# Loading the index queries ahead of the retention values, and preparing them one step sooner

## Chip, cores and metric

One core of one Trainium2 chip. The metric is the device time of one execution in microseconds (us), the median of several runs. A profiled execution gives the trace; times in it are counted from the start of its span.

## What is computed

One block of a language model on 512 tokens and 16 meta tokens (T = 528), width 1024, all in float32: a gated feed-forward layer, a mixer and a second feed-forward layer, each with a residual and a norm ahead of it. The mixer has two branches, a retention branch (4 heads, key width 256, value width 512) and a sparse attention branch (8 heads). In the sparse branch an index picks 128 keys for each query. The index is what is edited:

```python
def hybrid_mixer(u, pos, k_top, w_in, w_ret_out, w_att_out, w_mix_out):
    proj = u @ w_in
    rq, rk, rv, rg, aq, ak, av, iq, ik, iw, g_ret, g_att = jnp.split(proj, offs, axis=-1)
    ...
    yr = (jax.nn.silu(rg) * retention(rope(rq), rope(rk), rv)) @ w_ret_out
    iq = rope(iq.reshape(B, T, IDX_HEADS, IDX_DH), pos)      # 8 heads of 64
    ik = rope(ik.reshape(B, T, 1, IDX_DH), pos)[:, :, 0]
    ya = dsa_attention(aq, ak, av, iq, ik, iw, k_top).reshape(B, T, ATT_W) @ w_att_out
    merged = jax.nn.sigmoid(g_ret) * yr + jax.nn.sigmoid(g_att) * ya
    return merged @ w_mix_out

# in dsa_attention, for a block of queries:
    rel = jax.nn.relu(jnp.einsum('bqhd,bsd->bqhs', qib, ki))
    score = jnp.einsum('bqh,bqhs->bqs', wib, rel) * idx_scale
    _, sel = lax.top_k(score, k_top)
```

## The kernel before

Every product is made of three matmuls: both operands are split into a high and a low part (`hi`, `lo`), and high by high, high by low and low by high are summed. ACT makes the high part (a copy with rounding), DVE the low part (a subtraction). So each weight tile costs a load, an ACT split (`whi`) and a DVE split (`wlo`) before PE can use it.

The retention stage is one list of steps, run by `steps_through`. A step has a load, a tile of weights and a run. At step i the loop issues the load of step i+4, the ACT split of step i+2, and then the run of step i: its matmuls, then `lower()` (the DVE split of step i+2), then `behind(ps)` (what is done with the result). PE, ACT and DVE follow this written order; a scheduler orders the instructions of SP and POOL, which issue the transfers. Weight splits have three buffers, raw weights two (each two tiles), and the PSUM pool `sm` four banks.

The steps around the change are, in order:

- four gate tiles of head 0 (`psrg`; `gates_of(0)`). `behind_0` to `behind_3` apply silu; `behind_1` also computes head 0's decayed score matrix (`decayed(0)`, matmuls `psst`); `behind_1` to `behind_3` prepare the index queries; `behind_3` splits head 0's values (`values_in(0)`).
- two `psrq` tiles and two `psrk` tiles of head 1 (`queries_keys(1)`). `q0` prepares the index keys. `weigh(0, c)` multiplies values and score matrix (matmuls `pspv`), and DVE and ACT make `to`, `sq` and `ossum` from the result. `pair` calls put the index's own matmuls (`pssc`) between those of the projections.

The index queries wait in DRAM (`fq`). `bring_index`, called ahead of the first gate tile, loads them to `ia` (SP), and with the two halves of each head exchanged to `ib` (POOL, four pieces); it also loads the rope tables `cosi` and `sini`, head 0's values (four blocks, tile `vraw`), the index keys, the value tails and the causal mask. `index_queries(i)` has four parts:

- 0 multiplies `ia` by the cosine, 1 multiplies `ib` by the sine (DVE, 128 x 1536 each),
- 2 adds them (DVE) and copies the high parts to `iqx` (ACT, two copies of 64 x 1536),
- 3 subtracts for the low parts (DVE, two of 64 x 1536).

`index_keys(0)` to `(2)` are the same for the keys, with 64 x 512 elements. `ia` and `ib` share the memory of the value parts (`vo0`, `vo1`), so the values can be split only once the index queries are done. In the trace both appear as `ixs`.

Of the kernel before, what the change touches and what calls it, by code (L numbers as in the profile page):

```python
# [11 lines left out]
F32 = mybir.dt.float32  # L12
# [6 lines left out]
P = 128  # L19
D = 1024  # L20
KD = D // P
S = 512
# [59 lines left out]
def kernel(ctx: ExitStack, tc: tile.TileContext, x, meta, g1, wg1, wu1, wd1, gm,  # L82
                      w_in, w_ro, w_ao, w_mo, g2, wg2, wu2, wd2, gf, rope, decay, causal, out):
    nc = tc.nc
# [195 lines left out]
    vst = dpool.tile([6, P, 4, 4, P], F32, name="vst")  # L280
# [281 lines left out]
    if True:  # L562
# [120 lines left out]
        with tc.manual_schedule(engines={mybir.EngineType.PE, mybir.EngineType.Activation, mybir.EngineType.DVE}):  # L683
# [38 lines left out]
            second = [turned(1, (0,))]  # L722
# [66 lines left out]
        with tc.manual_schedule(engines=BUSY):  # L789
# [9 lines left out]
            raw = load_w(wg1[:, 2 * P : 4 * P], KD, 2 * P)  # L799
            w = split_w(raw[:, :, :P])  # L800
# [9 lines left out]
            w = split_w(raw[:, :, P:])  # L810
# [5 lines left out]
            lower = s1.hidden(0, pr)  # L816
            raw = load_w(wu1[:, 2 * P : 4 * P], KD, 2 * P)
# [3 lines left out]
            w = split_w(raw[:, :, :P])  # L821
# [6 lines left out]
            w = split_w(raw[:, :, P:])  # L828
# [58 lines left out]
        first, second = slice(0, 2 * P), slice(2 * P, 4 * P)  # L887
# [324 lines left out]
        with tc.manual_schedule(engines=BUSY):  # L1212
            pr = s1.spare("l", "pr")
            nc.vector.tensor_tensor(pr[:, 0, :], halves(psus[0])[1], st[0], ALU.mult)
            lower = s1.hidden(2, pr[:, 0, :], (0,))
# [156 lines left out]
    if True:  # L1372
# [4 lines left out]

        def bring_index():
            new_decay(0)
            heads[0]["raw"] = [rt.tile([P, S], F32, tag="to", name="vraw", bufs=4) for _ in range(4)]  # L1380
            for c in range(4):
                nc.sync.dma_start(heads[0]["raw"][c], vst[0, :, c].rearrange("p b d -> p (b d)"))
            nc.sync.dma_start(ia[:, :, :NL], fq[:, :, :NL])
            for r in range(4):
                o = r ^ 1
                nc.gpsimd.dma_start(ib[32 * r : 32 * r + 32, :, :NL], fq[32 * o : 32 * o + 32, :, :NL])
            for i, t in enumerate((cosi, sini)):
                nc.sync.dma_start(t, rope[0, i, :, REAL])
            nc.gpsimd.dma_start(ka[:64, :S], fs[:64, 0, :])
            for r in range(2):  # L1390
                nc.gpsimd.dma_start(kb_[32 * r : 32 * r + 32, :S], fs[32 * (1 - r) : 32 * (2 - r), 0, :])
            nc.gpsimd.dma_start(iw, fs[64 : 64 + IH, 0, :])
            place_tails(0)
            nc.sync.dma_start(caus, causal)
            for i, t in enumerate((cos, sin)):
                nc.sync.dma_start(t, rope[2, i])
# [5 lines left out]
        def index_queries(i):  # L1402
            late = slice(P, S)
            a, b = ia[:, :, :NL], ib[:, :, :NL]
            if i < 2:
                t, tb = ((a, cosi), (b, sini))[i]
                TT(t, t, tb[:, late].unsqueeze(1).to_broadcast([P, 4, NL]), ALU.mult)
            elif i == 2:
                TT(a, a, b, ALU.add)
                for r, own, far in sides_of:  # L1410
                    nc.scalar.activation(iqx[own, r::2, :], a[own], AF.Copy)
            else:
                for r, own, far in sides_of:
                    TT(iqx[far, r::2, :], a[own], iqx[own, r::2, :].bitcast(F32), ALU.subtract)

        def index_keys(i):
            a, b = ka[:64, :S], kb_[:64, :S]
            if i == 0:
                TT(a, a, cosi[:64], ALU.mult)
                TT(b, b, sini[:64], ALU.mult)  # L1420
            elif i == 1:
                TT(a, a, b, ALU.add)
                for r in (0, 64):
                    nc.scalar.activation(ikh[r : r + 64], a, AF.Copy)
            else:
                for r in (0, 64):
                    TT(ikl[r : r + 64], a, ikh[r : r + 64].bitcast(F32), ALU.subtract)
# [6 lines left out]
        def values_in(h):  # L1434
            if not vr.get("parts"):
                vr["parts"] = [rt.tile([P, 4, S], F32R, tag=f"vo{i}", name="vo") for i in range(2)]
            parts, raw = vr["parts"], heads[h]["raw"]
            if h == 0:
                lows = [in_two(raw[c], *(p[:, c, :] for p in parts)) for c in range(4)]
            else:  # L1440
                lows = [in_two(raw[:, c : c + 2], *(p[:, c : c + 2, :] for p in parts)) for c in (0, 2)]
            heads[h]["vs"] = [(parts[0][:, c, :], parts[1][:, c, :], tp["v"][:TR, c * P : (c + 1) * P]) for c in range(4)]
            for low in lows:
                low()
# [164 lines left out]
        def gates_of(h):  # L1609

            p = h - 1

            def behind_0(ps):
                silu(h, ps)
                if h:
                    norm_diag(p)
                    if h > 1:
                        pick(2)

            def behind_1(ps):  # L1620
                silu(h, ps)
                if h == 0:
                    decayed(0)
                    index_queries(0)
                else:
                    two_normed_parts(p, 0)

            def behind_2(ps):
                silu(h, ps)
                if h == 0:  # L1630
                    index_queries(1)
                    index_queries(2)
                elif h == 1:
                    two_normed_parts(p, 2)
                else:
                    pick(1)

            def behind_3(ps):
                silu(h, ps)
                if h == 0:  # L1640
                    index_queries(3)
                    values_in(0)
                    picks["pairs"] = index_steps()
                    picks["steps"] = select_steps()
                elif h == 1:
                    for _ in picks["pairs"]:
                        pass
                else:
                    if h == RH - 1:
                        weigh(h, 0)  # L1650
                    pick(3)

            sums, spread = (6, lambda: norm_sums(p)), (4, lambda: norm_all(p))
            inside = [()] * 4
            if h == 1:
                inside = [((2, pair), (4, pair), sums), ((1, pair), spread, (6, pair)), ((4, pair), (7, pair)),
                          ((4, pair),)]
            elif h:
                inside = [(sums,), ((4, lambda: pick(1)), (7, lambda: norm_all(p))), ((2, lambda: two_normed_parts(p, 2)),), ()]
            runs = [proj("psrg", REAL, i, b) for i, b in zip(inside, (behind_0, behind_1, behind_2, behind_3))]  # L1660
            if h == 0:
                run0 = runs[0]

                def first(w, lower):
                    bring_index()
                    run0(w, lower)

                runs[0] = first
            c0 = OFF_RG + h * DV
            if h < RH - 1:  # L1670
                return steps_of(tiles(("rg", h), w_in, c0, 4), runs)
            return steps_of(tiles(("rg", h), w_in, c0, 3) + tiles("rg3", w_in, c0 + 3 * P, 1), runs)

        def queries_keys(h):

            pss, p = {}, h - 1
            ropes = heads[h]["ropes"] = {}

            def q0(ps):
                pss["qa"] = ps  # L1680
                if h == 1:
                    for i in range(3):
                        index_keys(i)
                else:
                    weigh(p, 0)
                    pick(1)

            def q1(ps):
                pss["qb"] = ps
                ropes["q"] = rope_pieces(pss["qa"], ps, cos[:, REAL], sin[:, REAL], S, ret_q)  # L1690
                if h == 1:
                    weigh(p, 0)
                some(ropes["q"], 5)
                weigh(p, 1)
                if h > 1:
                    pick(1)

            def k0(ps):
                pss["ka"] = ps
                some(ropes["q"], 1)  # L1700
                weigh(p, 2)
                some(ropes["q"], 1)
                if h > 1:
                    pick(2)

            def k1(ps):
                ropes["k"] = rope_pieces(pss["ka"], ps, cos, sin, T, ret_k)
                weigh(p, 3)
                if h > 1:
                    pick(2)  # L1710

            inside = ((2, pair), (4, pair), (6, pair)) if h == 1 else ()
            return (steps_of(tiles(("rq", h), w_in, OFF_RQ + h * DK, 2), [proj("psrq", REAL, ((5, pair),) if h == 1 else (), q0), proj("psrq", REAL, (), q1)])
                    + steps_of(tiles(("rk", h), w_in, OFF_RK + h * DK, 2), [proj("psrk", None, (), k0), proj("psrk", None, inside, k1)]))

# [52 lines left out]
        p = RH - 1  # L1768
# [69 lines left out]
        raw = vr["raw"]  # L1838
# [465 lines left out]
```

## Time and profile before

| | |
|---|---|
| median of 3 runs | 1520.0 us (1519.72 to 1521.01) |
| the profiled execution | 1520.12 us, of which the span is 1518.3 us |
| PE busy | 1507.0 us (99%) |
| DVE busy | 1095.7 us (72%) |
| ACT busy | 722.2 us (48%) |
| POOL busy | 104.6 us (7%) |
| transfers | 173.48 MB, 114 GB/s over the span |

A row of a timeline has the start in us, the duration in us, the engine, the line of the kernel, the operation and its tiles, and in brackets the idle time of the engine just ahead of it with what ended that. A row of the waits has who waited, for whom, the sum in us, how often, and the longest. A row of the transfers has the issuing queue, the count, the size of each and the us from issue to landing. `SPq` and `POOLq` are the queues of SyncE and GpSimd.

### The profile page before, as it was taken

How to read it: one execution, taken by the hardware profiler on the slowest of the kernel's cores; microseconds unless marked ns; L12 is line 12 of the kernel's file. 1: busy time of each engine (PE TensorE's matmuls, PEld its weight loads, DVE VectorE, ACT ScalarE, POOL GpSimd, SP SyncE). 2: the span in 40 equal slices, each digit the busy share in tenths (PEclk: the TensorE clock that was granted, in tenths of full speed). 3: DMA queues.
4: the chain of work that ended last, by engine and by line, in shares of the span. 5: the costliest groups of instructions: out<-in, count | busy, mean ns of one | idle time of the engine just before them, and what ended most of it. 6: DMA issues, size and time to landing. Idle time of an engine off the chain costs nothing. (4 is left out here: it accounts for less than half of the span.)

```text
span 1518.3 us, 23905 instructions
## 1 busy us (share of the span) xinstructions
PE 1507.0 (99%) x9764; PEld 1370.3 (90%) x9764; DVE 1095.7 (72%) x1701; ACT 722.2 (48%) x1126; POOL 104.6 (7%) x136
## 2 busy tenths in 40 slices
PE   9999999999999999999999999999999999999997
PEld 8999999999988888889898888998888899899996
DVE  4988586786886767787878787666455888586675
ACT  5655263454354444543324357666344445254453
POOL 1000000003101120000000131110001000000000
PEclk9999999999999999999999999999999999999999
DMA  5232323226554444232322343333443223233232
GB/s 169 59 122 88 117 90 111 89 93 209 195 165 161 167 147 141 87 122 86 106 88 85 97 123 89 79 90 105 151 131 128 84 84 108 87 112 111 84 124 85
DMA packets 151741, 173.48 MB, mean 114 GB/s; under 512 B 4944, under 2 KB 123240, under 8 KB 150992
## 3 DMA queue, kind: packets, MB, share of 16 engines
q1 hardware_dynamic: 142992, 151.58, 31.8%
q0 software_dynamic: 3808, 11.38, 2.0%
q10 hardware_dynamic: 4832, 9.00, 1.7%
q8 instruction: 76, 1.25, 0.3%
q14 instruction: 33, 0.27, 0.1%
HBM read 155.94 MB, written 16.01 MB: 113 GB/s over the span
## 5 line engine op out<-in xcount | busy, mean ns | idle before, releaser
L303 ACT ACTIVATE whi<-raw 128x1024 fp32r<-128x1024 f32 (+2 forms) x184 | 169.8, 924 | 130.2 <-PE psd L157 37.3
L304 DVE TENSOR_TENSOR wlo<-raw,whi 128x1024 fp32r<-128x1024 f32 (+2 forms) x184 | 198.5, 1083 | 44.9 <-ACT whi L303 44.9
L157 PE MATMUL psqX<-tl,whi 128*128 128x264 f32 (+1 forms) x432 | 122.3, 283 | 0.0
L157 PE MATMUL psqX<-th,whi 128*128 128x264 f32 (+1 forms) x432 | 122.3, 283 | 0.0
L157 PE MATMUL psqX<-th,wlo 128*128 128x264 f32 (+1 forms) x432 | 122.2, 283 | 0.0
L118 DVE TENSOR_TENSOR wlo<-raw,whi 128x1024 fp32r<-128x1024 f32 (+1 forms) x60 | 73.6, 1226 | 54.3 <-ACT whi L117 51.8
L303 ACT ACTIVATE whi<-wsum 128x1024 fp32r<-128x1024 f32 x72 | 76.3, 1060 | 70.7 <-PE psd L2139 22.0
L117 ACT ACTIVATE whi<-raw 128x1024 fp32r<-128x1024 f32 (+1 forms) x60 | 62.3, 1043 | 87.5 <-PE psat L157 26.6
L304 DVE TENSOR_TENSOR wlo<-wsum,whi 128x1024 fp32r<-128x1024 f32 x72 | 87.7, 1219 | 12.5 <-ACT whi L303 12.5
L157 PEld LDWEIGHTS psqX<-th,whi 128*128 128x128 f32 x432 | 82.1, 190 | 0.1
L157 PEld LDWEIGHTS psqX<-th,wlo 128*128 128x128 f32 x432 | 82.0, 190 | 0.0
L157 PEld LDWEIGHTS psqX<-tl,whi 128*128 128x128 f32 x432 | 82.0, 190 | 0.0
L157 PE MATMUL psro<-vo,whi 128*128 128x512 f32 x256 | 78.8, 389 | 0.0
L157 PE MATMUL psd<-hl,whi 128*128 128x264 f32 x352 | 71.4, 284 | 0.0
L157 PE MATMUL psd<-hh,wlo 128*128 128x264 f32 x352 | 70.8, 283 | 0.0
L157 PE MATMUL psd<-hh,whi 128*128 128x264 f32 x352 | 70.6, 282 | 0.0
L2139 PE MATMUL psd<-wlo,hh 128*128 128x512 f32 (+1 forms) x182 | 69.3, 382 | 0.0
L2139 PE MATMUL psd<-whi,hh 128*128 128x512 f32 (+1 forms) x182 | 69.2, 382 | 0.0
L2139 PE MATMUL psd<-whi,hl 128*128 128x512 f32 (+1 forms) x182 | 69.2, 382 | 0.0
L157 PEld LDWEIGHTS psro<-vo,whi 128*128 128x128 f32 x256 | 48.1, 188 | 10.0
L157 PEld LDWEIGHTS psd<-hh,wlo 128*128 128x128 f32 x352 | 54.5, 188 | 0.0
L157 PEld LDWEIGHTS psd<-hh,whi 128*128 128x128 f32 x352 | 54.1, 188 | 0.0
(447 smaller groups left out, 4511.6 us busy)
## 6 DMA issues: line engine op xcount, KB each, us to landing
raw<-in_ffn_w_up_dram SPq DMA_DIRECT2D x22, 1024.0 KB, 5.2
raw<-in_ffn_w_gate_dram SPq DMA_DIRECT2D x21, 1024.0 KB, 5.1
raw<-in_w_in_dram SPq DMA_DIRECT2D x18, 1024.0 KB, 5.1
raw<-in_w_in_dram SPq DMA_DIRECT2D x33, 512.0 KB, 3.7
raw<-in_ffn_w_down_dram SPq DMA_DIRECT2D x24, 512.0 KB, 4.5
w<-in_w_in_dram SPq DMA_DIRECT2D x24, 512.0 KB, 6.3
raw<-in_ffn_w_down_dram SPq DMA_DIRECT2D x12, 768.0 KB, 4.5
raw<-in_w_ret_out_dram SPq DMA_DIRECT2D x8, 1024.0 KB, 5.1
```

Of the source, the lines that this page charges most:

```text
L117: nc.scalar.activation(hi, src, AF.Copy)
L118: eng.tensor_tensor(lo, src, hi.bitcast(F32), ALU.subtract)
L157: nc.tensor.matmul(o, a[:, k, :], b[:, sl], start=first and k == 0 and i == 0, stop=last and k == nk - 1 and i == 2, skip_group_check=onto)
L303: nc.scalar.activation(hi, src, AF.Copy)
L304: return lambda: nc.vector.tensor_tensor(lo, src, hi.bitcast(F32), ALU.subtract)
L2139: nc.tensor.matmul(ps, a[:, bs], m[:, j, cs], start=first and i == 0, stop=last and i == 2)
```

## The change

Three things move; no instruction is added or removed.

- The loads of the values, the index keys and weights, the value tails, the mask and the retention rope tables go from `bring_index` to a new `bring_more`, called ahead of the second gate tile. `bring_index` keeps the decay table, the index queries and their rope tables.
- The index query parts move up: 1 from `behind_2` to `behind_1`, 3 from `behind_3` to `behind_2`.
- The first part of the index keys moves from `q0` to `behind_3`.

```diff
         def bring_index():
             new_decay(0)
-            heads[0]["raw"] = [rt.tile([P, S], F32, tag="to", name="vraw", bufs=4) for _ in range(4)]
-            for c in range(4):
-                nc.sync.dma_start(heads[0]["raw"][c], vst[0, :, c].rearrange("p b d -> p (b d)"))
             nc.sync.dma_start(ia[:, :, :NL], fq[:, :, :NL])
             for r in range(4):
                 o = r ^ 1
                 nc.gpsimd.dma_start(ib[32 * r : 32 * r + 32, :, :NL], fq[32 * o : 32 * o + 32, :, :NL])
             for i, t in enumerate((cosi, sini)):
                 nc.sync.dma_start(t, rope[0, i, :, REAL])
+
+        def bring_more():
+
+            heads[0]["raw"] = [rt.tile([P, S], F32, tag="to", name="vraw", bufs=4) for _ in range(4)]
+            for c in range(4):
+                nc.sync.dma_start(heads[0]["raw"][c], vst[0, :, c].rearrange("p b d -> p (b d)"))
             nc.gpsimd.dma_start(ka[:64, :S], fs[:64, 0, :])
...
                 if h == 0:
                     decayed(0)
                     index_queries(0)
+                    index_queries(1)
...
                 if h == 0:
-                    index_queries(1)
                     index_queries(2)
+                    index_queries(3)
...
                 if h == 0:
-                    index_queries(3)
                     values_in(0)
+                    index_keys(0)
                     picks["pairs"] = index_steps()
...
                     run0(w, lower)
 
                 runs[0] = first
+                run1 = runs[1]
+
+                def second(w, lower):
+                    bring_more()
+                    run1(w, lower)
+
+                runs[1] = second
...
                 if h == 1:
-                    for i in range(3):
+                    for i in range(1, 3):
                         index_keys(i)
```

## The prediction

> **What bounds the kernel now.** I read the engine totals first, then who waited for whom on PE around the change, then PE, DVE and ACT in order of time there, then the transfers and their landing times.
>
> ```profile
> span 1518.3 us, 23905 instructions
> PE 1507.0 (99%) x9764; PEld 1370.3 (90%) x9764; DVE 1095.7 (72%) x1701; ACT 722.2 (48%) x1126; POOL 104.6 (7%) x136
> PE pssc L1290 <- ACT sq L271: 1.6, 1, 1.6
> PE psrq L157 <- DVE wlo L304: 0.5, 1, 0.5
> ```
>
> PE is busy for 99% of the span. The change cannot take matmuls away, so it can win only where PE stands still. These two waits lie in the stage that is edited; the only other one that the profile names on PE is at the kernel's first matmuls. Here they are on PE, with a start of the first `rq` tile and a regular pair ahead of them:
>
> ```profile
> 580.31 0.39 PE L157 MATMUL psrq<-xh,wlo 128*128 128x512 f32 x1
> 585.57 0.39 PE L157 MATMUL psrq<-xh,wlo 128*128 128x512 f32 x1
> 585.80 0.41 PE L157 MATMUL psrq<-xh,whi 128*128 128x512 f32 x1
> 586.05 0.39 PE L157 MATMUL psrq<-xl,whi 128*128 128x512 f32 x1
> 586.97 0.50 PE L157 MATMUL psrq<-xh,wlo 128*128 128x512 f32 x1 [0.54 <-DVE wlo L304]
> 587.31 0.40 PE L157 MATMUL psrq<-xh,whi 128*128 128x512 f32 x1
> 608.22 0.39 PE L1290 MATMUL pssc<-ikl,iq 128*128 128x512 f32 x1
> 610.25 0.50 PE L1290 MATMUL pssc<-ikh,iq 128*128 128x512 f32 x1 [1.64 <-ACT sq L271]
> 610.58 0.40 PE L1290 MATMUL pssc<-ikl,iq 128*128 128x512 f32 x1
> ```
>
> A 512-column matmul starts 0.23 us after the one before (585.57, 585.80). At 586.05 the next start comes 0.92 later (0.69 too late), and the one after it 0.34 later (0.11 too late): 0.80 us lost. At 608.22 it is 2.03 and then 0.33: 1.80 + 0.10 = 1.90 us. Together 2.70 us, which is all there is to win here.
>
> **Why PE waits there.** DVE and ACT run in the written order:
>
> ```profile
> 571.25 0.17 DVE L1345 TENSOR_TENSOR ptail<-tmp,ptail 16x16 fp32r<-16x16 f32 x1
> 575.10 1.76 DVE L1407 TENSOR_TENSOR ixs<-ixs,cos 128x1536 f32<-128x1536 f32 x1 [3.69 <-DMA cos<-in_rope_dram]
> 576.78 1.31 DVE L304 TENSOR_TENSOR wlo<-raw,whi 128x1024 fp32r<-128x1024 f32 x1
> 578.01 1.75 DVE L1407 TENSOR_TENSOR ixs<-ixs,sin 128x1536 f32<-128x1536 f32 x1
> 579.79 1.76 DVE L1409 TENSOR_TENSOR ixs<-ixs 128x1536 f32<-128x1536 f32 x1
> 581.59 2.98 ACT L1411 ACTIVATE iq<-ixs 64x1536 fp32r<-64x1536 f32 x2 [6.38 <-DVE ixs L1409]
> 584.60 1.06 ACT L303 ACTIVATE whi<-raw 128x1024 fp32r<-128x1024 f32 x1
> 585.69 1.23 DVE L304 TENSOR_TENSOR wlo<-raw,whi 128x1024 fp32r<-128x1024 f32 x1 [4.14 <-ACT whi L303]
> 586.95 3.52 DVE L1414 TENSOR_TENSOR iq<-ixs,iq 64x1536 fp32r<-64x1536 f32 x2
> 590.55 2.20 ACT L303 ACTIVATE vo<-vraw 128x512 fp32r<-128x512 f32 x4 [4.41 <-issue]
> 591.22 2.50 DVE L304 TENSOR_TENSOR vo<-vraw,vo 128x512 fp32r<-128x512 f32 x4 [0.75 <-ACT vo L303]
> 597.57 1.41 DVE L1427 TENSOR_TENSOR ikl<-tmp,ikh 64x512 fp32r<-64x512 f32 x2 [0.70 <-ACT ikh L1424]
> 600.46 0.68 DVE L1519 TENSOR_TENSOR to<-pspv,sg 128x512 f32<-128x512 f32 x1
> 608.82 0.68 DVE L1519 TENSOR_TENSOR to<-pspv,sg 128x512 f32<-128x512 f32 x1
> 609.60 0.60 ACT L271 ACTIVATE sq<-pspv 128x512 f32<-128x512 f32 x1
> ```
>
> DVE stands idle from 571.42 to 575.10 for the index rope table. The index copies on ACT (581.59 to 584.57) then hold back the weight split of the second `rq` tile (whi 584.60, wlo 585.69 to 586.92), and PE waits: the 0.80. The index work leaves DVE late for everything after it. The first `to` product starts at 600.46, the third at 608.82; its `sq` frees a PSUM bank (the `sm` pool has four) at 610.20, and PE takes that bank at 610.25: the 1.90.
>
> **The transfers.**
>
> ```profile
> u<-in_decay_dram SPq DMA_DIRECT2D x1, 384.0 KB, 7.2
> ixs<-fq SPq DMA_DIRECT2D x1, 768.0 KB, 15.8
> cos<-in_rope_dram SPq DMA_DIRECT2D x1, 256.0 KB, 14.9
> raw<-in_w_in_dram SPq DMA_DIRECT2D x1, 1024.0 KB, 14.2
> L1382 SPq DMA_DIRECT2D vraw<-vst x4: 376/444/545, 555.8 to 557.2; - x4
> DMA to landing us min/median/max: 4.9/7.9/13.2
> 555.01 0.65 SPq L1431 DMA_DIRECT2D u<-in_decay_dram  x1
> 558.67 0.61 SPq L1383 DMA_DIRECT2D ixs<-fq  x1
> 560.06 0.34 SPq L1388 DMA_DIRECT2D cos<-in_rope_dram  x1
> 564.72 0.62 SPq L133 DMA_DIRECT2D raw<-in_w_in_dram  x1
> ```
>
> Issue plus time to landing: the decay table at 562.2, the last value block at 557.2 + 13.2 = 570.4, the index queries (`ia`) at 574.5, the index cosine at 575.0 (DVE starts at 575.10), the next weights at 578.9. SP's transfers land in the order of their issue.
>
> On SP the built program moves only one thing: the four value loads now stand behind `ia`, cosine and sine. "One gate later" is the place in the code; no wait for the second gate is added. After the decay table SP brought 1024 KB by 570.4 (125 KB per us, beside POOL's loads), then 768 KB by 574.5 (187 KB per us). The same stream now carries `ia` first: 768 KB / 125 = 6.1 us, so 568.3; the cosine by 570.4; the sine 256 KB / 187 = 1.4 us later, at 571.8. DVE is free at 571.42, so the table wait (3.69 us) all but goes.
>
> The Trainium skill ("DMA: Bandwidth & Descriptors", section "Queues, rings and completion order") says that one engine consumes descriptors in ring order, but that completion is not first-in, first-out per issuing engine, as copies may spread over different numbers of rings. By this the tables might land with the values. The landings above are in order, so I forecast by them.
>
> The rest of the transfers: the next weights are issued when the slot eight transfers back is free, now at `ia`'s landing (568.3 instead of 564.7). SP still has 1.5 MB queued then, so they land near 578.9; ACT reads them after 585. The values land by about 577 and are split after 583. POOL's own order of work is the same. Cost of all this: nothing, with 5 us to spare.
>
> **The sums by step**, with the durations above. Multiply by cosine 571.4 to 573.2, by sine to 574.9. The split of the first `rq` tile, now behind both, ends at 576.2; PE wants it at 580.31. The sum ends at 577.9, the copies on ACT at 580.9, and whi of the second `rq` tile at 582.0. The lower index parts (3.52 on DVE) start after the first copy or after both: they end at 582.9 or 584.4. wlo of the second `rq` tile then ends at 584.2 or 585.7. PE wants it at 586.05 + 0.23 = 586.28: no wait, with 2.1 or 0.6 us to spare. Won: 0.80.
>
> The value split shares its buffers with the index queries, so it may start at 582.9 or 584.4 instead of 590.55: ACT 2.20, DVE done by about 588 at the latest, before PE reads the values at 591. The index keys' two products come one step sooner too; their last part ends at 592 to 593.5 instead of 598.98, so 5.5 to 7 us sooner. DVE then has the run from the first `to` to the third, 608.82 - 600.46 = 8.36 us, from about 594: the third could start at 602.4, but its own matmuls end only near 603.3. Its bank is free at about 604.6. PE asks for it at 608.45 - 0.80 = 607.65, three us later. Won: 1.90.
>
> What is late next? The weight splits have at least 0.6 us, and no other PE wait is named later. One side effect: the silu outputs and the value blocks change places in memory, and waits in the attention stage move between neighbouring ACT instructions. The work waited for is long over, so I take nothing:
>
> ```profile
> 875.16 3.53 POOL L1362 TENSOR_TENSOR accr<-accr,gate 128x512 f32<-128x512 f32 x2 [1.43 <-DVE accr L1746]
> 885.23 0.60 ACT L1266 ACTIVATE tmp<-psak 64x528 f32<-64x528 f32 x1 [5.47 <-PE psro L157]
> ```
>
> Sum: the profiled execution took 1520.12 us, 1.82 over its span and 0.12 over the median of the three runs. 1520.12 - 2.70 = **1517.4 us**.
>
> **The rivals.** *A: the tables come no sooner.* DVE starts at 575.1 as before, with the sine product now ahead of both splits. All moves by 3.7 us: wlo of the second `rq` tile ends at 587.9 to 589.4 and PE waits 1.6 to 3.1 us, 0.9 to 2.4 more than now. The bank is free at 607.6 to 608.8, while PE asks at 609.3 or later: the 1.90 goes. Net -1.0 to +0.5: 1519.1 to 1520.6. For it: POOL's index loads share the same engines. Against it: landing in order of issue. Chance 0.10.
>
> *B: slower.* The tables are served together with all that is queued and land with the last of it, at 578.9. DVE works in order, so the split of the first `rq` tile waits behind the index products until 578.9 + 4.8 = 583.7, 3.4 us after PE wants it. The second tile's split ends at 591.7 to 593.2, against a PE now due at 589.7: 2.0 to 3.5 more. 5.4 to 6.9 lost, 0.80 and 1.90 saved: +2.7 to +4.2, so 1522.8 to 1524.3. It decides from the start of the index work: above about 573 PE begins to wait, and between 574.7 and 576.2 the sum changes sign. Chance 0.08.
>
> The Trainium skill ("TensorE: Matmul & The Clock Gate", section "What's actually happening") puts the matmul clock at half after an idle window of about 3.4 us. By it B's first stall could cost some us more. No wait of the edited stage is that long in this trace.
>
> *C: only half of it.* Both index copies must end first and the tables slip a us: the wait at the second `rq` tile stays, the bank wait goes. 1520.12 - 1.90 = 1518.2. Chance 0.12.
>
> *D: nothing moves*, because the bank wait is replaced by one on the scores, which PE, ACT and DVE share: 1520.1. DVE's lead of over 5 us speaks against it. Chance 0.04.
>
> **How the numbers follow.** The forecast has 0.66. 0.2% is 3.04 us, about what a measurement of this kernel can tell from no change. The runs shown spread over 1.3 us, so a true 2.70 is measured past 3.04 in perhaps four cases of ten, and smaller waits that the table of waits leaves out may go as well: faster 0.28. Slower takes B with the spread of D and A: 0.10. The rest, 0.62, lies within. The range begins 0.9 below the forecast, for that spread and uncounted small waits, and ends at 1519.8, which takes in C and half of A; B, D and the rest of A are left out.
>
> **What would show it.** Right: cosine and `ia` land before 572, the DVE idle of 3.69 before the cosine product shrinks below 1, neither PE wait is named, the last index key part ends before 594, and the span is near 1515.6. Wrong in the first step: the cosine lands at 574 or later. Wrong in the second: a PE wait for wlo between 580 and 587. Wrong in the third: a PE wait for ACT `sq` stays near 607.

## The result, and the profile after

| | before | after | difference |
|---|---|---|---|
| median of 17 runs | 1519.72 us | 1516.58 us | -3.14 us; ratio 0.9979, 95% interval 0.9973 to 0.9986 |
| lowest and highest run | 1519.22, 1521.01 | 1516.23, 1517.68 | |
| span of the profiled execution | 1518.3 us | 1514.8 us | -3.5 us |

The changed kernel is faster by 0.21%, with an interval from 0.14% to 0.27%. The forecast was 1517.4, in a range from 1516.5 to 1519.8: the measured median lies within it, 0.08 us from its lower end.

The totals of the profile after, and all the PE waits that it names:

```profile
span 1514.8 us, 23904 instructions
PE 1505.7 (99%) x9764; PEld 1370.1 (90%) x9764; DVE 1096.0 (72%) x1701; ACT 722.2 (48%) x1126; POOL 104.6 (7%) x136
PE psg L627 <- DVE idle L595: 1.5, 1, 1.5
```

The work on each engine is what it was; the two PE waits of the edited stage are gone. To see what the stage itself gained, I take it from the start of the first gate tile to the start of the second norm sum (PE, before and then after), and beside it PE's busy time from 553 to 707 us:

```profile
553.89 0.39 PE L157 MATMUL psrg<-xh,whi 128*128 128x512 f32 x1
706.33 0.39 PE L1534 MATMUL psn<-ones,ossum 128*128 128x1 f32 x3
553.00:707.00 154.00, 151.82 (x830) 132.29 (x829) 110.07 (x167) 66.08 (x102) 13.19 (x28) 1.00 0.41 130
```

```profile
553.29 0.39 PE L157 MATMUL psrg<-xh,whi 128*128 128x512 f32 x1
702.94 0.50 PE L1537 MATMUL psn<-ones,ossum 128*128 128x1 f32 x4
553.00:707.00 154.00, 154.00 (x843) 134.80 (x842) 111.83 (x173) 67.85 (x104) 15.24 (x29) 1.00 0.40 130
```

The stage took 152.44 us and takes 149.65: **2.79 us less**. PE (the first number after the length) had 2.18 us idle in the window, the two waits of 0.54 and 1.64, and has none. What follows the stage is unchanged: 1518.3 - 706.33 = 811.97 before, 811.86 after. The rest of the difference between the two spans lies ahead of the stage (553.89 against 553.29), where both kernels have the same work.

The steps in order of time, DVE and ACT, after:

```profile
570.65 0.17 DVE L1345 TENSOR_TENSOR ptail<-tmp,ptail 16x16 fp32r<-16x16 f32 x1
570.84 1.76 DVE L1410 TENSOR_TENSOR ixs<-ixs,cos 128x1536 f32<-128x1536 f32 x1
572.52 1.75 DVE L1410 TENSOR_TENSOR ixs<-ixs,sin 128x1536 f32<-128x1536 f32 x1
574.19 1.22 DVE L304 TENSOR_TENSOR wlo<-raw,whi 128x1024 fp32r<-128x1024 f32 x1
577.11 3.00 ACT L1414 ACTIVATE iq<-ixs 64x1536 fp32r<-64x1536 f32 x2 [2.50 <-DVE ixs L1412]
578.63 3.54 DVE L1417 TENSOR_TENSOR iq<-ixs,iq 64x1536 fp32r<-64x1536 f32 x2 [1.55 <-ACT iq L1414]
582.21 1.23 DVE L304 TENSOR_TENSOR wlo<-raw,whi 128x1024 fp32r<-128x1024 f32 x1
585.65 0.39 PE L157 MATMUL psrq<-xh,wlo 128*128 128x512 f32 x1
589.47 1.41 DVE L1430 TENSOR_TENSOR ikl<-tmp,ikh 64x512 fp32r<-64x512 f32 x2 [0.70 <-ACT ikh L1427]
602.76 0.69 DVE L1522 TENSOR_TENSOR to<-pspv,sg 128x512 f32<-128x512 f32 x1 [1.48 <-PE pspv L1512]
603.55 0.60 ACT L271 ACTIVATE sq<-pspv 128x512 f32<-128x512 f32 x1 [1.60 <-DVE to L1522]
606.97 0.39 PE L1290 MATMUL pssc<-ikh,iq 128*128 128x512 f32 x1
```

DVE goes straight from the score matrix (ends 570.82) to the cosine product (570.84). The split of the second `rq` tile ends at 583.44, 2.2 us before PE uses it (585.65). The third `to` now waits 1.48 us for PE's `pspv`, where before it started late, with no idle time of DVE ahead of it; the bank is free at 604.15, and PE takes it at 606.97 without a wait.

### The profile page after: what moved, and what is told of

Read it like the earlier page. It is cut to its first block, busy times and chain, and to the rows that moved or that the text cites. A ratio compares the mean times of both kernels' runs of the same rounds, so it can differ in the third digit from the quotient of the medians.

```text
span 1514.8 us, 23904 instructions
## 1 busy us (share of the span) xinstructions
PE 1505.7 (99%) x9764; PEld 1370.1 (90%) x9764; DVE 1096.0 (72%) x1701; ACT 722.2 (48%) x1126; POOL 104.6 (7%) x136
## 4 chain that ended last, share of the span: by engine, by line
PE 99%; issue 0%; ACT 0%; DVE 0%; POOL 0%; POOLq 0%
PE psqX L157 14%; PE psd L157 8%; PE psd L2150 8%; PE psqY L157 7%; PE psrg L157 6%; PE psro L157 6%; PE psvX L1155 4%; PE psqZ L157 3%; PE psrk L157 3%; PE psak L157 3%; PE psu L157 3%; PE psrq L157 3%; PE psgate L157 3%; PE psaq L157 3%; PE psga L157 3%; PE psat L157 3%
```

## The experiments

All medians stand against runs of the kernel before on the same chip (1519.72 us beside the first runs of after, 1520.22 us beside e1, e2, e3 and e5; 1520.2 beside e4, e6 and the repeat of after). "Stage" is the stretch measured above, in the profiled execution.

| kernel | median us | ratio to before, 95% interval | stage us |
|---|---|---|---|
| before | | | 152.44 |
| after | 1516.58 | 0.9979 (0.9973 to 0.9986) | 149.65 |
| after, once more | 1517.07 | 0.9980 (0.9971 to 0.9989) | 149.65 |
| e1: loads alone | 1516.80 | 0.9979 (0.9970 to 0.9988) | 149.65 |
| e2: order alone | 1519.01 | 0.9992 (0.9983 to 1.0001) | 151.53 |
| e3: after, keys at their old step | 1517.28 | 0.9981 (0.9972 to 0.9989) | 149.65 |
| e5: after, old places in memory | 1517.07 | 0.9979 (0.9970 to 0.9988) | 149.65 |
| e4: new order, tables last | 1519.75 | 0.9997 (0.9988 to 1.0006) | 153.94 |
| e6: as e4, queries loaded twice | 1525.29 | 1.0031 (1.0019 to 1.0043) | 158.97 |

### e1: the loads alone

The loads as in the changed kernel, the index work in its old order:

```diff
                     index_queries(0)
-                    index_queries(1)
...
-                    index_queries(2)
-                    index_queries(3)
+                    index_queries(1)
+                    index_queries(2)
...
+                    index_queries(3)
                     values_in(0)
-                    index_keys(0)
...
-                    for i in range(1, 3):
+                    for i in range(3):
                         index_keys(i)
```

> The loads as after, the index work in the order of before. Theory (the table wait on DVE is the root of both PE waits): the tables land near 571, so the cosine product starts at once; the split of the first rq tile and then the sine product, sum and copies follow, wlo of the second rq tile ends near 583, 3 us before PE wants it; the last key part ends near 595 and the bank is free near 607, before PE asks. Both PE waits go: -2.7 us against before. Rival (the new place of the index work in the order is what counts): the index copies still stand ahead of the second tile's split, so no change, or at most -0.8.

Measured: ratio 0.9979, stage 149.65: the whole gain. The steps of this kernel that decide:

```profile
570.92 1.76 DVE L1410 TENSOR_TENSOR ixs<-ixs,cos 128x1536 f32<-128x1536 f32 x1
581.41 1.22 DVE L304 TENSOR_TENSOR wlo<-raw,whi 128x1024 fp32r<-128x1024 f32 x1 [4.13 <-ACT whi L303]
605.30 0.60 ACT L271 ACTIVATE sq<-pspv 128x512 f32<-128x512 f32 x1
607.04 0.39 PE L1290 MATMUL pssc<-ikh,iq 128*128 128x512 f32 x1
```

The tables are in time, so even the old order has the second split done at 582.63 and the bank free at 605.90, 1.1 us before PE takes it. The new order only moves slack: 2.8 us in place of 1.1 at the bank, and 0.8 us less at the second split, which after ends at 583.44. The rival that the order counts has fallen.

### e2: the order alone

The four moves of the index work on the kernel before, its loads unchanged:

```diff
                     index_queries(0)
+                    index_queries(1)
...
-                    index_queries(1)
                     index_queries(2)
+                    index_queries(3)
...
-                    index_queries(3)
                     values_in(0)
+                    index_keys(0)
...
-                    for i in range(3):
+                    for i in range(1, 3):
                         index_keys(i)
```

> The order of the index work as after, the loads as before. Theory: DVE starts the cosine product at 575.1 as before, wlo of the second rq tile ends 12.6 us later (as in the trace of after) at 587.7, 1.4 us after PE wants it; the bank wait goes, as the keys end near 595. Net -1.2 us. Rival (order counts): -2.7 us. Second rival (nothing without the loads): 0.

Measured: ratio 0.9992, 1.2 us less between the medians, with an interval from -2.6 to +0.2 us, so that the runs alone do not rule out no change; the stage of the profile is 0.91 us shorter, where -1.2 us was expected. The one PE wait that the profile names in the stage, and its cause:

```profile
PE psrq L157 <- DVE wlo L304: 1.5, 1, 1.5
575.79 1.76 DVE L1407 TENSOR_TENSOR ixs<-ixs,cos 128x1536 f32<-128x1536 f32 x1 [3.86 <-DMA cos<-in_rope_dram]
587.24 1.23 DVE L304 TENSOR_TENSOR wlo<-raw,whi 128x1024 fp32r<-128x1024 f32 x1
588.52 0.50 PE L157 MATMUL psrq<-xh,wlo 128*128 128x512 f32 x1 [1.50 <-DVE wlo L304]
```

DVE waits 3.86 us for the cosine table; wlo of the second `rq` tile ends 12.68 us after the cosine product starts (12.6 expected), and PE waits 1.50 where it had waited 0.54. The bank wait is gone. So the order trades a longer first wait for the second one; by the stage, that gives a third of what the loads give.

### e3 and e5: the two small parts

e3 takes `index_keys(0)` back to `q0`. e5 takes the value tiles from the pool in `bring_index`, so that values and silu outputs keep their old places:

```diff
                     values_in(0)
-                    index_keys(0)
...
-                    for i in range(1, 3):
+                    for i in range(3):
                         index_keys(i)
```

```diff
         def bring_index():
             new_decay(0)
+            heads[0]["raw"] = [rt.tile([P, S], F32, tag="to", name="vraw", bufs=4) for _ in range(4)]
...
         def bring_more():
-            heads[0]["raw"] = [rt.tile([P, S], F32, tag="to", name="vraw", bufs=4) for _ in range(4)]
```

> As after, but the first part of the index keys back at its old place. Theory: these two products lie in DVE's order next to where they were, with three us of slack at the bank: same as after, -3 us against before. Rival (the earlier keys remove the bank wait): only the first PE wait goes, -0.8 us, and the profile names a PE wait for sq near 604 to 608.

> As after, but the value tiles are taken from the pool ahead of the silu tiles, as before, so that they keep their old places in memory. Theory: places cost nothing, same as after, -3 us. Rival (the 0.4 us by which the measured gain of 3.14 is over the 2.70 counted on PE come from the new places): 0.4 us less gain than after, -2.7.

Measured: stage 149.65 in both, ratios 0.9981 and 0.9979. From the second norm sum to the end, the stretch with the attention stage, e5 takes 1515.3 - 703.35 = 811.95 us, against 811.86 after. Neither part matters once the tables are in time. The intervals of the medians are too wide to tell -2.7 from -3 us; the stage and the stretch behind it decide here.

### e4 and e6: how late the tables may be

e4 has the order of e2, and the tables behind values and mask. In e6 the added line that loads `ia` stands twice:

```diff
             for c in range(4):
                 nc.sync.dma_start(heads[0]["raw"][c], vst[0, :, c].rearrange("p b d -> p (b d)"))
-            nc.sync.dma_start(ia[:, :, :NL], fq[:, :, :NL])
...
-            for i, t in enumerate((cosi, sini)):
-                nc.sync.dma_start(t, rope[0, i, :, REAL])
...
             nc.sync.dma_start(caus, causal)
+            nc.sync.dma_start(ia[:, :, :NL], fq[:, :, :NL])
+            for i, t in enumerate((cosi, sini)):
+                nc.sync.dma_start(t, rope[0, i, :, REAL])
```

> The order of the index work as after, and the index queries and their rope tables loaded last of the group, behind the values and the mask (in the built order on SP: decay, values, mask, queries, cosine, sine). Theory (landing in order of issue; PE pays for each us by which the cosine product starts late): the 256 KB of the mask ahead of them put the start at 576.4 against 575.1; the split of the first rq tile ends 4.65 us later, 0.7 us after PE wants it, that of the second 12.7 us later, 2.1 us after the shifted PE wants it, the bank wait is gone. 2.9 lost against 2.70 lost before: +0.2 to +0.4 us. Rival B of the prediction (served together, landing with the last at 579): +2.7 to +4.2 us. Rival (the order alone brings the gain): -2.7 us.

> As e4, and the index queries are loaded a second time to the same tile, which waits for the first and stands behind the next weights on SP (768 KB more to load; the result is the same). Theory: the cosine product starts near 582, the split of the first rq tile ends 6.3 us after PE wants it, that of the second 2.1 us after the shifted PE wants it: 8.4 lost against 2.70: +5.7 us. Rival (a PE wait of over 3.4 us halves the matmul clock for some us): +7.5 to +9 us, and a granted clock below 1.00 behind the wait. Rival (late tables are hidden by the work of the first rq tile): under +3 us.

e4 measured no difference (ratio 0.9997, an interval from -1.8 to +0.9 us), where +0.2 to +0.4 us was expected; both rivals lie outside the interval. Its waits on PE, the start of the index work, two rows of the busy table (the granted TensorE clock is the third number from the right) and a matmul in it:

```profile
PE psrq L157 <- DVE wlo L304: 1.8, 2, 1.5
575.89 1.76 DVE L1407 TENSOR_TENSOR ixs<-ixs,cos 128x1536 f32<-128x1536 f32 x1 [4.75 <-DMA cos<-in_rope_dram]
588.00:589.00 1.00, 0.47 (x2) 0.43 (x3) 1.00 (x3) 1.00 (x3) 0.00 (x0) 1.00 0.00 0
591.00:592.00 1.00, 1.00 (x4) 0.81 (x3) 1.00 (x2) 0.00 (x0) 0.00 (x0) 0.50 1.08 376
590.09 0.63 PE L157 MATMUL psrq<-xl,whi 128*128 128x512 f32 x1
```

The start at 575.89, in a stage that began 0.27 us sooner, is 1.06 us later than before. PE waits twice, as the theory has it, but for 0.31 and 1.50 us, where the theory had it 0.7 and 2.1 us late. Its stage is 1.50 us longer than before all the same: after the waits the granted clock fell to 0.50 for about 3.4 us, and seven matmuls started 0.43 us apart instead of 0.23, which is 1.4 us. Without that the stage would be as long as before, within 0.1 us. In most other runs of e4 the mean clock was as high as in those of before (0.999 against 0.997 in this profile), and the median has little of it.

e6:

```profile
PE psrq L157 <- DVE wlo L304: 6.2, 1, 6.2
581.75 1.76 DVE L1408 TENSOR_TENSOR ixs<-ixs,cos 128x1536 f32<-128x1536 f32 x1 [10.66 <-DMA ixs<-fq]
582.00:584.00 2.00, 0.00 (x0) 0.00 (x0) 2.00 (x2) 0.00 (x0) 0.00 (x0) 0.58 0.00 0
588.00:590.00 2.00, 2.00 (x7) 1.52 (x6) 0.47 (x1) 1.96 (x2) 0.00 (x0) 0.50 0.00 0
592.00:594.00 2.00, 2.00 (x10) 1.55 (x10) 1.97 (x2) 1.47 (x4) 0.00 (x0) 0.86 0.00 0
```

The median is 5.1 us above before (1525.29 against 1520.2; by the ratio 2.9 to 6.5 us). PE waits 6.2 us for the first `rq` tile's split, as expected. The clock falls during the wait and is back some 6 us after it; PE, now slow, no longer waits for the second tile. So the clock cost took the place of the second wait, and the time is near the first theory (+5.7), below that of the rival (+7.5 to +9), although the clock did what the rival said. What the clock did is seen in one profile, that of the slowest of the six runs (1526.35 us); its stage is 6.5 us longer than before. The wait of 6.2 us rules out that late tables are hidden; the interval of the medians alone, from 2.9 us, just does not.

### After, once more

The changed kernel beside e4 and e6, with no edit.

> The changed kernel once more, beside the two others on one chip. Theory: the stage from the first gate tile to the second norm sum takes 149.65 us against 152.44 as in the first profile of after, and what the whole gain has above 2.79 us is scatter at the start of the kernel: -2.5 to -3.3 us. Rival (a further gain of about 0.4 us elsewhere): -3.1 us or more, with a stage after the second norm sum that is shorter too.

Measured: ratio 0.9980, 3.1 us less between the medians, which fits the theory and the rival, and stage 149.65 again; its profile has 1515.3 - 703.42 = 811.88 us from the second norm sum to the end, against 811.97 before and 811.86 after. The shorter stretch behind the stage, which the rival needs, is not there.

## Why the prediction was right

Times of after are 0.60 us ahead of those of before when the stage begins (553.29 against 553.89); with that added they can be laid beside the steps.

- **What can be won.** 2.70 us was counted on PE; the stage gained 2.79. From the first matmul of the first `rq` tile to the first `pspv` PE takes 592.11 - 579.85 = 12.26 us before and 590.64 - 579.25 = 11.39 after: 0.87 won, where 0.80 was counted. From the first `pssc` to the first norm sum it takes 622.48 - 605.60 = 16.88 us before and 619.10 - 604.13 = 14.97 after: 1.91 won, where 1.90 was counted. So the gain lies at the two waits and nowhere else in the stage.
- **The tables.** Cosine and sine were due at 570.4 and 571.8, `ia` at 568.3. The rows of after (issue, then the time to landing) give 570.10, 571.17 and 569.64, so 570.7, 571.8 and 570.2:

```profile
555.14 0.62 SPq L1380 DMA_DIRECT2D ixs<-fq  x1
556.00 0.61 SPq L1385 DMA_DIRECT2D cos<-in_rope_dram  x1
556.67 0.62 SPq L1385 DMA_DIRECT2D sin<-in_rope_dram  x1
ixs<-fq SPq DMA_DIRECT2D x1, 768.0 KB, 14.5
cos<-in_rope_dram SPq DMA_DIRECT2D x1, 256.0 KB, 14.1
sin<-in_rope_dram SPq DMA_DIRECT2D x1, 256.0 KB, 14.5
```

  `ia` came 1.9 us later than worked out and close to the cosine, so the stream was not a strict row of one transfer after the other. It cost nothing, since the cosine was last in any case. On landing in the order of issue the trace decided rightly: the Trainium skill ("DMA: Bandwidth & Descriptors", section "Queues, rings and completion order") allows another order of completion, and none was seen among these three.
- **The split of the second `rq` tile.** Due to end at 584.2 or 585.7, ended at 583.44 + 0.60 = 584.0: the lower parts start after the first of the two copies. PE had 2.2 us to spare (2.1 forecast).
- **The bank.** Due free at 604.6 and asked for at 607.65; free at 604.75, taken at 607.57.
- **The rest of the transfers and the places in memory**, taken at nothing: e5 confirms the places; no wait for the next weights appeared. The next weights were issued at 569.70, right behind the landing of `ia` (569.64), and took 9.5 us, so they landed at 579.2, or 579.8 in the clock of before (578.9 worked out); ACT first read them at 584.31.
- **Rival A** (tables no sooner) was tried as e2: -1.0 to +0.5 was given, the stage shows -0.9 and the medians -1.2. **Rival B**'s threshold was given as a start between 574.7 and 576.2, where the sum changes sign: e4's start lies at 576.16 in the clock of before, and its stage, without the slow clock, was equal to before within 0.1. B's own start, 579, was not tried. In e6 the work starts 3 us later still (581.75 + 0.32 = 582.07 in that clock) and the stage is 6.5 us longer, in part by the slow clock: lateness costs time of that order, but B's own figures were not shown.

Of the signs that the prediction named, only the span came out otherwise: 1514.8 us instead of 1515.6. Of the 3.5 us between the two spans 2.79 lie in the stage, 0.60 ahead of it and 0.11 behind it.

Two things the prediction did not see. It priced the order alone (rival A), but never the loads alone, and those carry all of the gain (e1). And the chances put most weight within 0.2%; the measured 0.21% lies just beyond that line, with an interval that covers both sides. That the median still lies within the range owes something to luck: it is 0.84 us under 1520.12 - 2.70. Of that, 0.40 come from the start of the sum, one execution of 1520.12 us where the median of 17 runs is 1519.72, and 0.44 from a gain of 3.14 between the medians, of which the stage shows 2.79.

Open is the difference between the 2.79 us of the stage and the 2.9 to 3.4 us between the medians of the kernels with the same stage. The start of the stage scatters from 553.3 to 554.4 us over the profiles, with the same work ahead of it, and each interval covers 2.79. But all five medians lie beyond it, so scatter alone is not shown to be the reason; whether anything else is gained was not shown.

## What to carry to other kernels

When a busy engine's few waits all trace back to data that reach another engine late, put the transfers of those data first in the queue and see how far that alone goes, before work is reordered. Here the order cost nothing once its data were in time: e1 and after have the same stage. Count the gain on the bound engine by its own start times, in the stage that is edited; here that gave 2.70 of 2.79 us.

## What the runs showed of the hardware

In the profile of e4, waits of 0.31 and 1.50 us, 8 us apart, were followed by a granted clock of 0.50 from about 589.4 to 592.8, for 3.4 us; in e2 one wait of 1.50 us, and in before one of 1.64, were not. Why one was and the others were not is open. In e6 the clock fell at about 582.3, some 2.2 us after PE's last matmul ahead of the 6.2 us wait had ended, and was back at about 592.5, after 10.2 us. The Trainium skill ("TensorE: Matmul & The Clock Gate", section "What's actually happening") speaks of an idle window of about 3.4 us, running freely. The lengths of the two falls, 3.4 and 10.2 us, are one and three such windows; but in neither profile had PE stood idle for 3.4 us when its clock fell.
